# TensorE's order written out from layer C's output projection to block 2's first gate values

## The chip, the core and the metric

One core of one Trainium2 chip runs the whole program, a transformer of two blocks, in one launch. The metric is the device time of one execution in microseconds (us), the median of three runs: 2364.74 us, between 2364.59 and 2366.53. Engines are named as the profile names them: PE (TensorE, the matrix products; PEld its weight loads), DVE (VectorE), ACT (ScalarE), POOL (GpSimd) and SP (SyncE, whose queue issues the loads).

## The reference, cut to what matters

Layer C ends block 1: each head's output is normalised, gated and projected, and a layer norm with a residual follows. Block 2 begins with an RMS norm of the result and projects it; one of the projections gives `zv`, the values of a spatial gate, which go through a GELU and a layer norm.

```python
def hgrn2_readout(o, g, g_norm, w_out):
    on = o * lax.rsqrt(jnp.mean(o * o, axis=-1, keepdims=True) + RMS_EPS) * g_norm
    B, H, L, dv = on.shape
    return (on.transpose(0, 2, 1, 3).reshape(B, L, H * dv).astype(g.dtype) * jax.nn.silu(g)) @ w_out
...
    y = hgrn2_readout(o_f + o_b, g, g_norm, w_out)
    x_new = layer_norm(DEEPNORM_ALPHA * x + gate * y, ln_g, ln_b)
...
        a = rms_norm(h, pre_mix_g[i])
        z = a @ w_in[i]
...
    v = layer_norm_2(jax.nn.gelu(v), ln_g, ln_b)
```

There are 512 tokens, 1024 channels and 8 heads in layer C.

## The kernel before, in words

Activations lie with their channels on the 128 partitions, in 8 tiles k of 128 channels, and the 512 tokens run along the free axis; most work is done in two halves of 256 tokens (`HALVES`). A product is computed in three parts, `mm3` (line 269) and its stepwise form `mm3_steps` (274): each weight and each operand is split into an upper and a lower part, and upper x upper, upper x lower and lower x upper are summed, 3 products for each of the 8 k, so 24 for one output tile of 128 channels. They all carry line 279. `wsplit` (241) loads a weight (line 238, SP's queue), copies its upper part on ACT (246) and takes the lower part on DVE (249). There are 4 buffers for loaded weights and 3 for each split part.

The program is written down in Python and ordered by a list scheduler that simulates the engines: each engine's instructions are put in the order in which the simulation finds them ready, the earlier written first. Inside `with self.tc.manual_schedule(engines={PE})` PE's instructions are prescribed in the order in which they are written; the other engines' are still ordered by the scheduler. Before the change two parts use it: the attention of block 1, and the attention of block 2 with what follows it (`mixer`). There a `_Slots` object (188) holds "sides": generators whose steps are advanced by one at each call `slot(...)`, so that small products come at fixed places between large ones.

The part that changes is `c_out`. `head_out` (line 964) finishes a head of layer C: transposes (975), the states (983, 985), the output products (989 to 991), the head norm (995 to 998), a transpose (1001) and the gate (1002). `c_out` splits the eight heads' outputs into `oh` (line 253 on ACT, 254 on DVE; the profile calls them `hx`). For each half it computes 8 output tiles m; three weights (m = 3, 4, 5) are kept from half 0 in spare buffers (`kw`), so that half 1 starts with these. A result gets its gate and the residual on DVE (1029), and the sum over the tiles is formed on POOL, the last addition on DVE (1031, `total`).

Then come two norms for each half. The layer norm (`layer_norm_steps`, 423): PE's product with a matrix of 1/1024 gives the mean (434, `mu`), DVE subtracts it (439), ACT squares (440), DVE adds the squares (458); `rstd` sums them over channels by 8 small products (312, `rsc`), DVE adds the epsilon (315), POOL takes the power -0.5 (316, `rcol`), PE spreads it over the partitions (320, `rsb`), and DVE multiplies (446). Gain and bias are applied twice: on ACT inside the squares for the next norm (466), and on POOL in place, eight times (1044). The second norm, block 2's RMS norm (`norm_out`), has the same `rstd` chain (312 to 320) and `normed` (1076), which multiplies on DVE (1081) and splits into `self.a`, the upper part on ACT (253), the lower on DVE and POOL in turn (254).

`mixer_in` begins block 2. Its constants are loaded first (lines 1243 to 1255). `token_major` (834) computes the gate values of token tiles 0 and 1, that is of half 0: 4 weights, 2 tiles, 6 products each of 512 columns (line 845), in PSUM tiles `mm`, and `gln_evac` passes them on. `group` (1120) follows: five output tiles of other projections, first for half 0, then for half 1. PE's order in all this is the scheduler's.

Of the kernel before, what the change touches and what calls it, by code (L numbers as in the profile page):

```python
# [10 lines left out]
F32 = mybir.dt.float32  # L11
# [3 lines left out]
AF = mybir.ActivationFunctionType  # L15
ALU = mybir.AluOpType
# [5 lines left out]
ALPHA = 4 ** 0.25  # L22
LN_EPS, RMS_EPS = 1e-5, 1e-6
NORM_EPS = 1e-6
NEG = -1e30
HALVES = [slice(0, 256), slice(256, 512)]
# [152 lines left out]
def now(steps):  # L179

    while True:
        try:
            next(steps)
        except StopIteration as e:
            return e.value
# [21 lines left out]
class _K:  # L207
# [796 lines left out]
    def c_out(self, cp):  # L1004

        nc = self.nc
        nrm = self.nrm
        oh = self.new_x()
        for sl in HALVES:
            for k in range(8):  # L1010
                self.split(oh[0][:, k, sl], oh[1][:, k, sl], self.oy[:, k, sl])
        kept = {}
        kw = [[self.te.tile([128, 1024], F32R, name="kw", tag=t, bufs=b) for _ in range(2)]
              for t, b in (("kqc", 3), ("kq", 2), ("ff", 2))]

        for hf, sl in enumerate(HALVES):
            bank = ("o", "pt")[hf]
            total = cp.tile([128, 256], F32, name="total", tag="total", bufs=2)
            order = range(8)
            if hf:  # L1020
                order = [*kept, *(m for m in range(8) if m not in kept)]
            for i, m in enumerate(order):
                w = (kept.pop(m) if m in kept else self.wsplit(self.d["wo_c"][m])) if hf or not 3 <= m < 6 else None
                if w is None:
                    w = kept[m] = self.wsplit(self.d["wo_c"][m], *kw.pop())
                p = self.big((128, 256))
                self.mm3(p, w, [lambda k, t=t: t[:, k, sl] for t in oh])
                r = self.h[:, m, sl]
                nc.vector.scalar_tensor_tensor(r, p, self.mod[:, 40 + m, 0:1], r, op0=ALU.mult, op1=ALU.add)
                if i:  # L1030
                    (nc.vector if i == 7 else nc.gpsimd).tensor_add(total, total if i > 1 else first, r)
                first = r
            r = self.h[:, :, sl]

            def squares(i, t):
                next(steps)
                for j in range(2):
                    self.gain_bias(r[:, 2 * i + j, :], 2 * i + j, 1, t[:, j, :], AF.Square)

            steps = self.layer_norm_steps(r, 1, cp, lambda k, xn: None, [total], bank, "lq")  # L1040
            next(steps)
            sq = self.sumsq(squares, 256, nrm)
            for k in range(8):
                nc.gpsimd.tensor_scalar(r[:, k, :], r[:, k, :], self.c("ln_g", 8 + k), self.c("ln_b", 8 + k), op0=ALU.mult,
                                        op1=ALU.add)
            self.norm_out(nrm, "pre_mix", 0, sl, sq, bank)


    def norm_in(self, tmp, gain, l, sl, dst=None):
# [175 lines left out]
    def mixer_in(self, l, at, gp, u, qst, kst, kcst, vv, vcz, gt):  # L1225

        nc, d = self.nc, self.d
# [56 lines left out]
        def gln_evac(t, n, p):  # L1284
            x = v[:, t, :]
            self.gelu2(x, p, gp.tile([128, S], F32, name="gmt", tag="gmt", bufs=2))
            bst = gp.tile([128, 6], F32, name="bst", tag="bst", bufs=2)
            mv = gp.tile([128, 2], F32, name="mv", tag="mv", bufs=2)
            nc.vector.bn_stats(bst, x)
            nc.vector.bn_aggr(mv, bst)  # L1290
            nc.gpsimd.tensor_scalar(mv[:, 1:2], mv[:, 1:2], 4 * NORM_EPS, None, op0=ALU.add)
            nc.gpsimd.tensor_tensor(mv[:, 1:2], mv[:, 1:2], self.mhalf[:, 0:1], op=ALU.pow)
            nc.vector.tensor_scalar(x, x, mv[:, 0:1], mv[:, 1:2], op0=ALU.subtract, op1=ALU.mult)
            eng = nc.vector if t < 2 else nc.gpsimd
            eng.tensor_mul(x, x, gln[0])
            eng.tensor_add(x, x, gln[1])

        zv = lambda ts, bank: self.token_major(d[f"w_zv{l}"], 1, lambda k, b, t: self.a[b][:, k, 128 * t:128 * t + 128], ts,
                                               bank, gln_evac)
        zv((0, 1), lambda: self.bk("mm", [128, 512]))  # L1300
        order = (0, 1, 6, 7, 8)
        wgs = [at.tile([128, 192], F32R, name=f"wgs{i}") for i in range(2)]
        self.split(wgs[0], wgs[1], wg)
# [16 lines left out]
        for b in range(2):  # L1320
            k_ = roped(gr[6 + b], 1.0)
            for g in range(2):
                x, y = (slice(0, 64), slice(64, 128)) if g == 0 else (slice(64, 128), slice(0, 64))
# [16 lines left out]
        for r in range(4):  # L1340
            q_ = roped(proj(8 + r) if r else gr[8], 0.125)
            compress(r)
            for g in range(2):
                x, y = (slice(0, 64), slice(64, 128)) if g == 0 else (slice(64, 128), slice(0, 64))
                nc.scalar.copy(qst[x, 2 * r + g, :], q_[x, :])
                nc.vector.tensor_sub(qst[y, 2 * r + g, :], q_[x, :], qst[x, 2 * r + g, :])
        for b in range(2):
            v_ = ev("v_")
            nc.scalar.copy(v_, proj(12 + b))
            p = ptt("vtr", [128, 4, 128])  # L1350
# [6 lines left out]
        p = ptt("htr", [128, 2, 128])  # L1357
# [4 lines left out]
        p = ptt("pkc", [128, 64])  # L1362
# [9 lines left out]
        p = ptt("pvc", [31, 2, 64])  # L1372
# [7 lines left out]
        p = ptt("gtr", [128, 4, 24])  # L1380
# [341 lines left out]
```

## Time and profile before

| | |
|---|---|
| median of three runs | 2364.74 us |
| the profiled execution | 2362.37 us |
| its span, first to last instruction | 2360.5 us |
| PE busy | 2237.1 us |
| DVE busy | 1701.1 us |
| ACT busy | 1140.2 us |
| POOL busy | 519.6 us |
| mean granted PE clock (1 is full speed) | 0.981 |

Times in the rows are microseconds from the span's start unless marked ns. A timeline row gives start, duration, engine, line, operation, out<-in, shape and count; in brackets stands how long the engine sat idle before it and what ended the wait. Consecutive instructions of one kind are merged into one row. PE's products overlap in the pipe, so a row's duration holds the last one's whole length. "PEclk" is the clock that PE was granted: 1.00 is 2.4 GHz, 0.50 is 1.2 GHz.

### The profile page before, as it was taken

Reading aid. Unit: us, or ns where it says so; the run is one execution under the profiler, and the core shown is the slowest. Engines: PE = TensorE matmul, PEld = TensorE weight load, DVE = VectorE, ACT = ScalarE, POOL = GpSimd, SP = SyncE. Lnnn points to the kernel's source line nnn. Section 1 sums busy time; section 2 is a strip of 40 time slices with the busy share of each in tenths; the row PEclk is TensorE's granted clock in tenths of the full one; section 3 lists DMA queues with packets and bytes.
Section 4 is the critical chain, followed back from the end, with each engine's and each line's share of the span. In section 5 each row is a group of like instructions: output and inputs, shape, how many; then the busy total and the mean of one; then the engine's idle time right before and its main releaser. Section 6 shows DMA issues by size and latency. Waiting matters only on the chain.

```text
span 2360.5 us, 37236 instructions
## 1 busy us (share of the span) xinstructions
PE 2237.1 (95%) x14372; PEld 1941.6 (82%) x14372; DVE 1701.1 (72%) x2922; ACT 1140.2 (48%) x2105; POOL 519.6 (22%) x556
## 2 busy tenths in 40 slices
PE   7999999999999989897999999999987999999998
PEld 5877788888888888665898889998865798888998
DVE  5898656846888878776787665668957688666558
ACT  3534444643443434455664444555445665444454
POOL 0110010312444344113121110133203131111004
PEclk9999999999999999998999999999988999999999
DMA  7443134432212344311253235655411143333664
GB/s 286 134 151 99 37 104 132 141 124 82 62 63 63 113 152 130 132 37 46 81 170 105 92 95 157 181 185 163 176 53 45 43 157 126 96 98 112 176 195 134
DMA packets 83746, 279.03 MB, mean 118 GB/s; under 512 B 9584, under 2 KB 14704, under 8 KB 83568
## 3 DMA queue, kind: packets, MB, share of 16 engines
q1 hardware_dynamic: 83568, 276.64, 36.7%
q8 instruction: 113, 1.85, 0.3%
q14 instruction: 65, 0.53, 0.1%
HBM read 274.51 MB, written 2.10 MB: 117 GB/s over the span
## 4 chain that ended last, share of the span: by engine, by line
PE 75%; DVE 13%; ACT 4%; issue 3%; POOL 3%; DMA 2%; SPq 0%; DVEq 0%; ACTq 0%; POOLq 0%
PE mm L279 28%; PE bg L279 23%; PE s L279 3%; DVE wlo L249 2%; PE o L580 2%; PE s L924 2%; PE pt L571 2%; PE bg L845 2%; PE pt L279 1%; PE s L1558 1%; DMA w<-in_w_ada 1%; ACT whi L246 1%; PE s L845 1%; PE bg L1659 1%; DVE ada_p L403 1%
## 5 line engine op out<-in xcount | busy, mean ns | idle before, releaser
L246 ACT CAST whi<-w 128x1024 fp32r<-128x1024 f32 (+1 forms) x436 | 449.1, 1033 | 555.5 <-PE mm L279 249.0
L249 DVE TENSOR_TENSOR wlo<-w,whi 128x1024 fp32r<-128x1024 f32 (+1 forms) x420 | 522.7, 1246 | 223.6 <-ACT whi L246 221.7
L279 PE MATMUL bg<-a,whi 128*128 128x512 f32 x1344 | 415.9, 391 | 0.2 <-ACT whi L246 0.2
L279 PEld LDWEIGHTS bg<-a,whi 128*128 128x128 f32 x1344 | 252.3, 188 | 54.6 <-ACT whi L246 1.0
L279 PE MATMUL mm<-hx,whi 128*128 128x512 f32 x864 | 275.6, 399 | 3.4 <-DVE sga L682 3.0
L279 PE MATMUL bg<-a,wlo 128*128 128x512 f32 x672 | 262.2, 391 | 2.0 <-DVE wlo L249 2.0
L279 PE MATMUL mm<-fh,whi 128*128 128x256 f32 x1408 | 252.7, 282 | 0.0
L279 PEld LDWEIGHTS mm<-fh,whi 128*128 128x128 f32 x1408 | 217.2, 189 | 0.2
L279 PE MATMUL mm<-fh,wlo 128*128 128x256 f32 x704 | 198.9, 284 | 0.6 <-DVE wlo L249 0.6
L279 PEld LDWEIGHTS mm<-hx,whi 128*128 128x128 f32 x864 | 157.9, 190 | 33.1 <-DVE sga L682 3.2
L279 PE MATMUL mm<-a,whi 128*128 128x256 f32 (+1 forms) x768 | 169.8, 317 | 0.0
L279 PE MATMUL mm<-hx,wlo 128*128 128x512 f32 x432 | 169.7, 393 | 0.0
L279 PEld LDWEIGHTS bg<-a,wlo 128*128 128x128 f32 x672 | 126.6, 188 | 29.8 <-DVE wlo L249 3.1
L1611 POOL TENSOR_TENSOR cv<-cv 128x512 f32<-128x512 f32 x44 | 61.5, 1398 | 386.2 <-DVE cv L1598 386.2
L1598 DVE SCALAR_TENSOR_TENSOR cv<-q,cols,cv 128x511 f32<-128x511 f32 (+1 forms) x176 | 134.5, 767 | 2.5
L279 PEld LDWEIGHTS mm<-fh,wlo 128*128 128x128 f32 x704 | 132.6, 189 | 1.0 <-DVE wlo L249 1.0
L279 PEld LDWEIGHTS mm<-a,whi 128*128 128x128 f32 x768 | 124.0, 196 | 7.1 <-issue 4.2
L1605 DVE TENSOR_TENSOR q<-bg,rr 128x512 f32<-128x512 f32 x74 | 51.1, 691 | 107.6 <-PE bg L279 107.6
L279 PE MATMUL mm<-a,wlo 128*128 128x256 f32 (+1 forms) x384 | 117.8, 307 | 0.6 <-DVE wlo L249 0.6
L279 PE MATMUL mm<-hc,whi 128*128 128x256 f32 x576 | 108.6, 287 | 2.3 <-ACT k L813 2.2
L316 POOL TENSOR_TENSOR rcol<-rcol,mhalf 128x2 f32<-128x2 f32 x33 | 24.3, 736 | 348.4 <-DVE rcol L315 348.4
L571 PE MATMUL pt<-ident,p 128*128 128x128 f32 x496 | 72.8, 285 | 29.4 <-DVE p L1577 20.8
(465 smaller groups left out, 4999.8 us busy)
## 6 DMA issues: line engine op xcount, KB each, us to landing
w<-in_wup SPq DMA_DIRECT2D x102, 512.0 KB, 3.5
w<-in_wdn SPq DMA_DIRECT2D x64, 448.0 KB, 3.5
w<-in_w_ada SPq DMA_DIRECT2D x48, 512.0 KB, 3.7
w<-in_w_c SPq DMA_DIRECT2D x48, 512.0 KB, 3.5
w<-in_w_in SPq DMA_DIRECT2D x38, 512.0 KB, 4.7
w<-in_wo SPq DMA_DIRECT2D x32, 512.0 KB, 3.5
w<-in_wdn SPq DMA_DIRECT2D x32, 512.0 KB, 3.6
w<-in_wpg SPq DMA_DIRECT2D x32, 512.0 KB, 3.8
```

The costliest lines, as they stand in the source:

```text
L246: self.nc.scalar.copy(hi[:, :c], w)
L249: eng.tensor_sub(lo[:, :c], w, hi[:, :c])
L279: self.nc.tensor.matmul(ps, w[a][:, (k - k0) * c:(k - k0 + 1) * c], x[b](k), start=first and n == 0, stop=last and n == 3 * len(ks) - 1)
L316: nc.gpsimd.tensor_tensor(col, col, self.mhalf[:, :nt], op=ALU.pow)
L403: nc.vector.scalar_tensor_tensor(t, w, 1.0, self.srow[i], op0=ALU.mult, op1=ALU.mult, accum_out=sums[:, j, i:i + 1])
L571: nc.tensor.transpose(pt[:, c:c + 128], P[g][:, i, kb * 128:(kb + 1) * 128], self.ident)
L580: self.nc.tensor.matmul(o[64 * g:64 * g + 64, 2 * rp:2 * rp + 2, :].rearrange("p a b -> p (a b)"), vt[:, keys[kb], 64 * g:64 * g + 64], pb ...
L845: nc.tensor.matmul(p, xf(k, a, t), w[b][:, 512 * k2:512 * k2 + 512], start=k == 0 and i == 0, stop=k == 7 and i == 2)
L924: nc.tensor.matmul(s_[:, c, :], lhs(c), rhs(c), start=True, stop=True)
L1598: nc.vector.scalar_tensor_tensor(t[:, s:], p[:, :S - s], cw(i), t[:, s:], op0=ALU.mult, op1=ALU.add)
L1605: nc.vector.tensor_mul(q, p, self.rr)
L1611: nc.gpsimd.tensor_mul(a, a, b)
```

## The change

PE's instructions of `c_out` are prescribed, and the gate values of half 0 are moved into that stretch. In each half the tiles' products are written whole, tile by tile and k from 0 to 7, with a slot after every 12 products (`k % 4 == 3`), so two for each tile. After a half its norms become a side, a new generator `norms`. Its first step waits; the next slot gives the mean's product; after the squares four more steps pass; then come the eight small products of the first `rstd`, one slot later its broadcast; after the squares of the second norm five steps pass; then the second `rstd` in two slots. So half 0's norms run through the 16 slots of half 1: mean at slot 1, sums at slot 5, broadcast at 6, sums of the second norm at 11, its broadcast at 12. Half 1's norms run in the 8 slots of the gate values, one after each 6 products; what is left of them (from the second norm's sums on) is written after the prescribed stretch and stays free. The gate values take their weights through `wqueue`, which splits one weight ahead; their PSUM tiles are kept in `self.zv`, and `mixer_in` only calls `gln_evac` on them in the first of block 2's layers. In the second layer nothing changes. The instructions and their number are the same.

```diff
-        for hf, sl in enumerate(HALVES):
-            bank = ("o", "pt")[hf]
-            total = cp.tile([128, 256], F32, name="total", tag="total", bufs=2)
-            order = range(8)
-            if hf:
-                order = [*kept, *(m for m in range(8) if m not in kept)]
-            for i, m in enumerate(order):
...
-                p = self.big((128, 256))
-                self.mm3(p, w, [lambda k, t=t: t[:, k, sl] for t in oh])
...
+        def norms(sl, total, bank):
+
             r = self.h[:, :, sl]
+            pair = lambda i: r[:, 2 * i:2 * i + 2, :]
+            both = lambda t: t[:, None, :].to_broadcast([128, 2, 256])
+            yield
+            mu = self.bk(bank, [128, 256], "mu")
+            nc.tensor.matmul(mu, self.mean1k, total, start=True, stop=True)
+
+            def centred(i, t):
+                nc.vector.tensor_sub(pair(i), pair(i), both(mu))
+                nc.scalar.activation(t, pair(i), AF.Square)
+
+            sq = self.sumsq(centred, 256, cp, "lq")
+            for _ in range(4):
+                yield
+            rs = yield from self.rstd_steps(sq, 256, self.mean1k, LN_EPS / ALPHA ** 2, cp, bank)
 
             def squares(i, t):
-                next(steps)
+                nc.vector.tensor_mul(pair(i), pair(i), both(rs))
                 for j in range(2):
                     self.gain_bias(r[:, 2 * i + j, :], 2 * i + j, 1, t[:, j, :], AF.Square)
 
-            steps = self.layer_norm_steps(r, 1, cp, lambda k, xn: None, [total], bank, "lq")
-            next(steps)
             sq = self.sumsq(squares, 256, nrm)
             for k in range(8):
                 nc.gpsimd.tensor_scalar(r[:, k, :], r[:, k, :], self.c("ln_g", 8 + k), self.c("ln_b", 8 + k), op0=ALU.mult,
                                         op1=ALU.add)
-            self.norm_out(nrm, "pre_mix", 0, sl, sq, bank)
+            for _ in range(5):
+                yield
+            pr = yield from self.rstd_steps(sq, 256, self.mean1k, NORM_EPS, nrm, bank)
+            self.normed(nrm, pr, lambda k: self.h[:, k, sl], lambda k: self.c("pre_mix", k), range(8), sl)
+
+        slot = _Slots()
+        with self.tc.manual_schedule(engines={mybir.EngineType.PE}):
+            for hf, sl in enumerate(HALVES):
...
+                for i, m in enumerate(order):
...
+                    p = self.big((128, 256))
+                    for k, _ in enumerate(self.mm3_steps(p, w, [lambda k, t=t: t[:, k, sl] for t in oh])):
+                        if k % 4 == 3:
+                            slot(0)
...
+                slot.side(norms(sl, total, ("o", "pt")[hf]))
+
+            self.zv = [self.bk("mm", [128, 512]) for _ in range(2)]
+            wq = self.wqueue([self.d["w_zv0"][0, k] for k in range(4)])
+            for kq in range(4):
+                w = next(wq)
+                for t, p in enumerate(self.zv):
+                    for k in (2 * kq, 2 * kq + 1):
+                        for i, (a, b) in enumerate(((0, 0), (0, 1), (1, 0))):
+                            nc.tensor.matmul(p, self.a[a][:, k, 128 * t:128 * t + 128], w[b][:, 512 * (k % 2):512 * (k % 2) + 512],
+                                             start=k == 0 and i == 0, stop=k == 7 and i == 2)
+                    slot(0)
+        for x in slot.sides:
+            now(x)
...
-        zv((0, 1), lambda: self.bk("mm", [128, 512]))
+        if l == 0:
+            for t, p in enumerate(self.zv):
+                gln_evac(t, 0, p)
+        else:
+            zv((0, 1), lambda: self.bk("mm", [128, 512]))
```

## Rows read from the trace of the kernel before

**Rows 1.** The page, part 1: busy us, share of the span, instructions.

```profile
PE 2237.1 (95%) x14372; PEld 1941.6 (82%) x14372; DVE 1701.1 (72%) x2922; ACT 1140.2 (48%) x2105; POOL 519.6 (22%) x556
```

**Rows 2.** Busy time by stretch: the projection, and what follows it.

```profile
core 0: us, PE busy (x) PEld busy (x) DVE busy (x) ACT busy (x) POOL busy (x), PEclk, DMA share, GB/s
839.40:874.60 35.20, 35.13 (x291) 35.00 (x291) 27.72 (x40) 15.55 (x23) 15.91 (x17) 1.00 0.37 113
874.60:893.20 18.60, 8.85 (x32) 6.06 (x30) 16.75 (x27) 7.04 (x15) 16.04 (x17) 0.63 0.50 173
```

**Rows 3.** Timeline of PE, 874 to 892: the products behind a wait.

```profile
876.04 1.02 PE L312 MATMUL rsc<-mean1k,nq 128*128 128x1 f32 x8 [1.32 <-DVE nq L458]
879.11 1.22 PE L434 MATMUL mu<-total,mean1k 128*128 128x256 f32 x2 [2.05 <-DVE total L1031]
883.05 0.69 PE L320 MATMUL rsb<-ident,rcol 128*128 128x128 f32 x2 [2.72 <-POOL rcol L316]
884.75 0.80 PE L845 MATMUL mm<-whi,a 128*128 128x512 f32 x1 [1.01 <-ACT a L253]
...
889.48 1.22 PE L845 MATMUL mm<-whi,a 128*128 128x512 f32 x2 [2.66 <-DVE a L254]
```

**Rows 4.** Busy time in two stretches of 2 us; PEclk is the third number from the end.

```profile
878.00:880.00 2.00, 0.89 (x2) 0.50 (x2) 1.37 (x2) 0.00 (x0) 2.00 (x3) 0.75 0.87 180
...
892.00:894.00 2.00, 2.00 (x12) 1.78 (x12) 1.62 (x3) 0.37 (x1) 1.52 (x3) 0.84 0.00 0
```

**Rows 5.** Timeline of PE where block 2's prescribed attention begins.

```profile
979.36 0.56 PE L1558 MATMUL s<-kst,qst 128*128 128x128 f32 x4
979.75 0.62 PE L1352 MATMUL vtr<-ident,v__9486 128*128 128x128 f32 x4
```

**Rows 6.** Groups of PE's products, 805 to 839.45: those of the projection.

```profile
L279 PE MATMUL bg<-hx,whi 128*128 128x256 f32 x42 | 8.2, 291 | 0.4 <-ACT whi L246 0.3
L279 PE MATMUL bg<-hx,wlo 128*128 128x256 f32 x21 | 5.9, 287 | 0.0
L279 PE MATMUL bg<-hx,kw 128*128 128x256 f32 x42 | 5.4, 285 | 0.0
```

**Rows 7.** Timeline of PE while head 7 is finished.

```profile
822.95 0.60 PE L975 MATMUL pt<-ident,KK 128*128 128x128 f32 x4
...
829.49 2.56 PE L279 MATMUL bg<-hx,kw 128*128 128x256 f32 x20
831.89 0.38 PE L991 MATMUL o<-st,QQ 128*128 128x128 f32 x2
```

**Rows 8.** Timelines of ACT (first row) and DVE, the same stretch.

```profile
825.60 0.58 ACT L977 COPY kt<-pt 128x512 f32<-128x512 f32 x1
...
827.20 1.23 DVE L249 TENSOR_TENSOR kw<-w,kw 128x1024 fp32r<-128x1024 f32 x1
828.34 1.75 DVE L985 SCALAR_TENSOR_TENSOR st<-st,F,pt 128x128 f32<-128x128 f32 x5
```

**Rows 9.** Timelines of PE, DVE and POOL: half 0's norms.

```profile
868.22 0.38 PE L320 MATMUL rsb<-ident,rcol 128*128 128x128 f32 x2
...
875.22 0.68 DVE L458 TENSOR_TENSOR nq<-nq 128x512 f32<-128x512 f32 x1
...
870.59 2.59 POOL L1044 TENSOR_SCALAR h<-h,cols 128x256 f32<-128x256 f32 x3 [3.31 <-ACT nq L466]
873.15 1.20 POOL L1031 TENSOR_TENSOR total<-total,h 128x256 f32<-128x256 f32 x1
874.33 3.58 POOL L1044 TENSOR_SCALAR h<-h,cols 128x256 f32<-128x256 f32 x3
...
878.59 2.31 POOL L1044 TENSOR_SCALAR h<-h,cols 128x256 f32<-128x256 f32 x2
...
882.28 0.72 POOL L316 TENSOR_TENSOR rcol<-rcol,mhalf 128x2 f32<-128x2 f32 x1
```

**Rows 10.** Timeline of SP's queue: loads of the gate values' weights.

```profile
851.72 16.99 SPq L238 DMA_DIRECT2D w<-in_w_zv x4
```

**Rows 11.** Line 1044: durations in ns, shortest/median/longest.

```profile
L1044 POOL TENSOR_SCALAR h<-h,cols x16: 549/982/2062, 870.6 to 908.5; 128x256 f32<-128x256 f32 x16
```

More of the change, by code (lines that the diff above doesn't have):

```diff
@@ L1014, in c_out @@
               for t, b in (("kqc", 3), ("kq", 2), ("ff", 2))]
-        for hf, sl in enumerate(HALVES):
-            bank = ("o", "pt")[hf]
-            total = cp.tile([128, 256], F32, name="total", tag="total", bufs=2)
-            order = range(8)
-            if hf:
-                order = [*kept, *(m for m in range(8) if m not in kept)]
-            for i, m in enumerate(order):
-                w = (kept.pop(m) if m in kept else self.wsplit(self.d["wo_c"][m])) if hf or not 3 <= m < 6 else None
-                if w is None:
-                    w = kept[m] = self.wsplit(self.d["wo_c"][m], *kw.pop())
-                p = self.big((128, 256))
-                self.mm3(p, w, [lambda k, t=t: t[:, k, sl] for t in oh])
[L1028 to L1032, printed above, removed]
-            r = self.h[:, :, sl]
+        def norms(sl, total, bank):
+            r = self.h[:, :, sl]
+            pair = lambda i: r[:, 2 * i:2 * i + 2, :]
[10 more added lines that the diff above has]
+            rs = yield from self.rstd_steps(sq, 256, self.mean1k, LN_EPS / ALPHA ** 2, cp, bank)
             def squares(i, t):
-                next(steps)
+                nc.vector.tensor_mul(pair(i), pair(i), both(rs))
                 for j in range(2):
                     self.gain_bias(r[:, 2 * i + j, :], 2 * i + j, 1, t[:, j, :], AF.Square)
-            steps = self.layer_norm_steps(r, 1, cp, lambda k, xn: None, [total], bank, "lq")
-            next(steps)
             sq = self.sumsq(squares, 256, nrm)
@@ L1045, in c_out @@
                                         op1=ALU.add)
-            self.norm_out(nrm, "pre_mix", 0, sl, sq, bank)
+            for _ in range(5):
[5 more added lines that the diff above has]
+            for hf, sl in enumerate(HALVES):
+                total = cp.tile([128, 256], F32, name="total", tag="total", bufs=2)
+                order = [*kept, *(m for m in range(8) if m not in kept)]
+                for i, m in enumerate(order):
+                    w = (kept.pop(m) if m in kept else self.wsplit(self.d["wo_c"][m])) if hf or not 3 <= m < 6 else None
+                    if w is None:
+                        w = kept[m] = self.wsplit(self.d["wo_c"][m], *kw.pop())
+                    p = self.big((128, 256))
+                    for k, _ in enumerate(self.mm3_steps(p, w, [lambda k, t=t: t[:, k, sl] for t in oh])):
+                        if k % 4 == 3:
+                            slot(0)
+                    r = self.h[:, m, sl]
+                    nc.vector.scalar_tensor_tensor(r, p, self.mod[:, 40 + m, 0:1], r, op0=ALU.mult, op1=ALU.add)
+                    if i:
+                        (nc.vector if i == 7 else nc.gpsimd).tensor_add(total, total if i > 1 else first, r)
+                    first = r
+                slot.side(norms(sl, total, ("o", "pt")[hf]))
[11 more added lines that the diff above has]
+            now(x)
     def norm_in(self, tmp, gain, l, sl, dst=None):
```

## The prediction

> **What bounds the kernel now.** The page comes first: TensorE (PE) is busy 95% of the span [rows 1], so only a stretch where PE is not full can give time back. The busy time by stretch shows one in the code that changes. While layer C's output projection runs PE is full (35.13 of 35.2 us); in the 18.6 us behind it PE works 8.85 us at a mean clock of 0.63 [rows 2]. PE's timeline says why. The products that end half 0's norms and begin half 1's come one at a time, each behind VectorE (DVE), ScalarE (ACT) or GpSimd (POOL). The bracketed idle times are 1.32, 2.05, 2.72, 1.01 and 2.66 us, together 9.8 us [rows 3]. The granted clock fell in this hole: a mean of 0.75 in 878 to 880 puts the fall to half speed at 879.0, and 0.84 in 892 to 894 puts the rise at 892.6 [rows 4]. In these 13.6 us PE waited 6.4 us (the last three waits) and worked about 7.2 us at 1.2 instead of 2.4 GHz, which cost half of that, 3.6 us. **The hole is worth 9.8 + 3.6 = 13.4 us**: all that the change can win here.
>
> **What the order binds.** The change issues the same instructions; only PE's order is prescribed. The kernel has such a stretch elsewhere. In it the attention scores (line 1558, inside the prescribed order) run at 979.36, ahead of a transpose of line 1352 that is written earlier and lies outside it [rows 5]. So prescribed instructions keep their order among themselves, and free ones are put between them as they come ready. The last head's products (lines 975 to 1001) are free and stay where they are; layer C's projection becomes prescribed.
>
> **Cost 1: the work ahead of the last head.** Today the projection does not wait for head 7. Of the first five output tiles the 21 products with k = 0 to 6 (7 k, 3 products each) are already issued while head 7 is being finished: 42 + 21 + 42 = 105 [rows 6]. In the prescribed order tile 0's k = 7 comes 22nd, and it needs head 7's output. So 21 products go ahead and 84 move behind. A group of 20 takes 2.56 us [rows 7]; with 0.28 for the last, that is (2.56 - 0.28)/19 = 0.12 us apart. 84 x 0.12 = **10.1 us move from a covered place to the path**.
>
> Does head 7 come sooner without them? Its last products (lines 989 to 991) start at 831.89, behind a group that ran from 829.49 [rows 7]. Their operand, the state (line 985), is ready at 828.34 + 1.75 = 830.09, and that chain is set by DVE and ACT, not by PE: the copy of the turned keys (line 977) at 825.60 and a weight's lower part (line 249) at 827.20 stand ahead of it in their engines' order [rows 8]. I expect this order to stay, as PE held nothing that these instructions wait for. So head 7 gains 831.89 - 830.09 = **1.8 us**. Bounds: nothing, if the order of the others shifts against it; 5.8 us, if the key copy followed its transposes at once (822.95 + 0.60 = 823.55 [rows 7]): copy 0.58 [rows 8], six products 0.9 (the four transposes' 0.60 x 6/4), three states at 1.75/5 = 0.35 each, so the state is ready at 826.1, which is 4.0 before 830.09, and 4.0 + 1.8 = 5.8. I take 1.8, as every row on the chain but PE's keeps its place.
>
> Without its fillers PE does only short pieces from 823.6 until head 7's output is there. In the hole above the clock fell at 879.0, after a stop at 876.04 - 1.32 = 874.7 and 1.0 us of work in between [rows 3, 4], so I expect it to fall here, and the projection to start at half speed. After the restart at 889.48 PE was at half speed until 892.6 [rows 3, 4], which loses 1.6 us; bounds 0 and 3.6, the hole's own loss. I take **1.6**. Sum of cost 1: 10.1 - 1.8 + 1.6 = 9.9 us.
>
> **Cost 2: a wait at a set place.** In half 1 a slot comes every 12 products, 12 x 0.12 = 1.44 us. The first norm's mean comes at slot 1, its sums at slot 5, its broadcast at slot 6, the second norm's sums at slot 11, its broadcast at slot 12; each is now a fixed point behind which PE's other products queue. Before, the broadcast was done at 868.22 + 0.38 = 868.60 and the last sum of squares at 875.22 + 0.68 = 875.90 [rows 9], 7.3 us later; five slots give 7.2, so slot 11 hardly waits. Slot 12 does. Its broadcast needs POOL's power (line 316), and POOL has eight affines of line 1044 ahead of it: 870.59 (2.0 us after the broadcast) to 878.59 + 2.31 = 880.90, 10.3 us with two additions of line 1031 between them [rows 9]. The power takes 0.72 [rows 9], so it is ready 2.0 + 10.3 + 0.7 = 13.0 us after the broadcast. PE gets there after 7.2 + 1.0 (the eight small products, 1.02 [rows 3]) + 1.44 = 9.6. It waits **3.4 us**, with the rest of half 1 behind it, and half 1's last sum and so its own norms wait too. Bounds: zero with affines near their shortest, and 6.2 (rival 2).
>
> **Cost 3: the smaller set places.** Slots 1, 5 and 6 of both halves. The nearest rows are the waits of the same products today, 2.05 and 1.32 [rows 3]; they were long since DVE and POOL did two things at once. I take **1.8 us** for all six; bounds 0 and 3.4 (both in full).
>
> **Costed at nothing.** The gate values' four weights were issued to SP's queue from 851.72 on, for 17 us [rows 10], ahead of block 2's constants though written behind them, and were there before the gate values began at 884.75 [rows 3]; so writing them ahead of the constants moves them past nothing. If they came later, the gate values would begin later. The products of the gate values, 48, and the norms are the same number. The end of the second half's norms stays free, as before, and is covered by the five tiles that follow; if it came late, those would wait for half 1 of `a`.
>
> **The sum.** Costs 9.9 + 3.4 + 1.8 = 15.1 us against 13.4 us from the hole: **1.7 us slower**. The profiled execution took 2362.37 us (its span 2360.5 and 1.9 around it), so 2364.1 in its terms; the median of the three runs, 2364.74, is 2.4 above it, so **2366.4 us**. A measurement of this kernel can tell about 0.2%, 4.7 us: this is no change.
>
> **A rule on POOL.** First the row: line 1044 takes 549 ns at the shortest, 982 at the median, 2062 at the longest, for one shape [rows 11]. The Trainium skill (SBUF — State Buffer, section Who interferes with whom) says that a VectorE instruction with two SBUF inputs and a GpSimd instruction that reads SBUF share a read interface, so that the later one waits for the whole of the earlier. By that rule the spread in the row is waiting, with which the trace agrees as far as it goes, and the time would be near rival 2's; that price is worked out from rows alone.
>
> **Rivals.**
> 1. *Faster: head 7 really comes sooner.* If ACT and DVE serve head 7 first, cost 1 is 10.1 - 5.8 + 1.6 = 5.9. If besides POOL's affines run near 0.55 us [rows 11], POOL needs 8 x 0.55 + 2 x 1.20 (the addition at 873.15 [rows 9]) = 6.8, its power is ready at 2.0 + 6.8 + 0.7 = 9.5 and slot 12 waits for nothing; with 1.0 for the small places the costs are 6.9, the gain 6.5, the time 2358.2. For it: PE is free for head 7. Against: [rows 8]. Chance 0.22.
> 2. *Slower: GpSimd sets the pace of half 1.* The place is slot 12. Prescribed, half 1 runs its additions beside the affines; three lie among them instead of two. The three affines from 874.33 took 3.58/3 = 1.19 each and the addition before them 1.20 [rows 9]: 8 x 1.19 + 3 x 1.2 = 13.1, so the power comes at 15.8 and PE waits 6.2 us. That is longer than the 4.3 us from the stop to the clock's fall in the hole [rows 3, 4], so 1.6 us more. 1.7 + (6.2 - 3.4) + 1.6 = 6.1 us slower, 2370.8. It decides from the point where the last affine ends over 13 us after the broadcast, when the wait passes 4 us. For it: these affines lay beside a loaded DVE, as they would. Against: the first three, from 870.59, took only 2.59/3 = 0.86. Chance 0.30.
> 3. *The order does less than it says.* The free parts set the end: half 1's `a` comes as late as before and the five tiles wait for it, or PE's order comes out nearly the same. Then 2364.7. Against: the 105 products ahead of time can't stay. Chance 0.05.
>
> The forecast itself has 0.43. **How the numbers follow.** Forecast and rival 3 are within 0.2%: 0.48. Rival 1 gives faster 0.22, rival 2 slower 0.30. The forecast's own range, with costs 2 and 3 between their bounds in part, is 2362 to 2370. The range reaches to rival 1's 2358 and past rival 2's 2370.8 to 2372.5, since the costs' upper bounds (clock 3.6, small places 3.4) can add to it.
>
> **What would show it.** Cost 1: few products of line 279 with `bg<-hx` before head 7's output, some 21, PE idle ahead of lines 991 and 1001, the clock below 1.00 there. Cost 2: one wait of line 320 for POOL `rcol` inside half 1, 2 to 5 us. The hole: no stretch of 18 us with half-busy PE behind the projection. I am wrong if line 991's products start well before 830 on this clock, if that wait is missing, or if PE still idles before the gate values.

## The result: 0.6% slower, 2381.53 us

The changed kernel takes 2381.53 us (median of four runs, 2376.37 to 2383.24); the kernel before, beside it, 2365.64. The ratio is 1.0061, 95% interval 1.0043 to 1.0080. The forecast, 2366.4 with a range up to 2372.5, is wrong: the loss is outside the range.

The first part of the page hardly moves; PE's busy time is 13 us longer than in [rows 1] for the same 14372 instructions, so some of them ran at a lower clock:

```profile
PE 2250.0 (95%) x14372; PEld 1952.8 (82%) x14372; DVE 1699.6 (71%) x2922; ACT 1141.0 (48%) x2105; POOL 519.0 (22%) x556
```

**By stretch.** PE's busy time in the changed kernel (columns: stretch, its length, PE busy with its instructions, granted clock, DMA share, GB/s). The projection, which ran full at 1.00 in [rows 2], now starts behind a half-empty stretch, and its first 15 us have a mean clock of 0.81. The hole of [rows 2] between 875 and 893 is gone (18.47 of 20 us busy), but a new one has opened in the gate values, 895 to 910.

```profile
820.00:840.00 20.00, 10.35 (x65) 0.80 0.57 192
840.00:855.00 15.00, 15.00 (x103) 0.81 0.38 119
855.00:875.00 20.00, 19.03 (x150) 0.95 0.18 53
875.00:895.00 20.00, 18.47 (x142) 0.97 0.33 95
895.00:910.00 15.00, 8.75 (x38) 0.90 0.68 210
910.00:935.00 25.00, 25.00 (x168) 0.85 0.53 155
```

**Head 7.** The groups of the projection's products, 805 to 839.9, are 14 + 7 = 21 where [rows 6] had 105. These are the groups:

```profile
L279 PE MATMUL bg<-hx,whi 128*128 128x256 f32 x14 | 2.7, 290 | 0.0
L279 PE MATMUL bg<-hx,wlo 128*128 128x256 f32 x7 | 2.1, 298 | 0.4 <-DVE wlo L249 0.4
```

PE now stands and waits (its timeline) where [rows 7] showed it working:

```profile
826.68 0.94 PE L983 MATMUL pt<-iv,kt 128*128 128x128 f32 x6 [2.15 <-ACT kt L977]
830.15 0.79 PE L991 MATMUL o<-st,QQ 128*128 128x128 f32 x2 [2.53 <-DVE st L985]
...
838.12 0.63 PE L1001 MATMUL pt<-ident,on 128*128 128x128 f32 x4 [3.34 <-DVE on L998]
839.97 1.04 PE L279 MATMUL bg<-hx,whi 128*128 128x256 f32 x2 [1.22 <-ACT hx L253]
```

The last products of head 7 start at 830.15, 1.7 us before the 831.89 of [rows 7]. But the clock has just fallen, and it falls a second time where the projection begins (the windows of PE again):

```profile
826.00:828.00 2.00, 0.94 (x6) 1.00 0.97 371
828.00:830.00 2.00, 0.00 (x0) 0.63 0.92 320
830.00:834.00 4.00, 3.85 (x18) 0.50 0.54 171
836.00:838.00 2.00, 0.00 (x0) 1.00 0.00 0
838.00:840.00 2.00, 0.66 (x5) 0.69 0.00 0
840.00:844.00 4.00, 4.00 (x17) 0.50 0.17 53
844.00:846.00 2.00, 2.00 (x12) 0.60 0.72 190
```

Two products take 0.79 us instead of 0.38, and head 7's output is there at 839.97, not sooner than the 839.47 of the kernel before (its timeline of PE):

```profile
839.47 0.62 PE L279 MATMUL bg<-hx,whi 128*128 128x256 f32 x3 [1.22 <-ACT hx L253]
```

**Half 1.** POOL's affines and its power (line 1041 is the old 1044) answer to [rows 9] (timeline of POOL):

```profile
877.54 2.18 POOL L1041 TENSOR_SCALAR h<-h,cols 128x256 f32<-128x256 f32 x4 [0.49 <-ACT nq L466]
880.85 5.25 POOL L1041 TENSOR_SCALAR h<-h,cols 128x256 f32<-128x256 f32 x4
886.75 0.71 POOL L316 TENSOR_TENSOR rcol<-rcol,mhalf 128x2 f32<-128x2 f32 x1
```

Beside them DVE did this (its timeline):

```profile
876.11 2.48 DVE L1035 TENSOR_TENSOR h<-h,rsb 128x512 f32<-128x512 f32 x4
...
879.55 1.86 DVE L458 TENSOR_TENSOR nq<-nq 128x512 f32<-128x512 f32 x2
881.33 1.21 DVE L249 TENSOR_TENSOR wlo<-w,whi 128x1024 fp32r<-128x1024 f32 x1
...
883.46 1.21 DVE L249 TENSOR_TENSOR wlo<-w,whi 128x1024 fp32r<-128x1024 f32 x1
```

PE waited at slots 5, 11 and 12 (its timeline):

```profile
871.92 1.02 PE L312 MATMUL rsc<-mean1k,nq 128*128 128x1 f32 x8 [0.97 <-DVE nq L458]
883.68 1.02 PE L312 MATMUL rsc<-mean1k,nq 128*128 128x1 f32 x8 [0.26 <-DVE nq L458]
887.51 0.43 PE L320 MATMUL rsb<-ident,rcol 128*128 128x128 f32 x2 [1.27 <-POOL rcol L316]
```

**The gate values.** They begin at 893.52 and end at 920.6, 27 us for 48 products (timeline of PE; each of the 48 takes 0.23 at full clock, together 11 us). The mean of half 1, at slot 1, waits 3.59 us. Then 24 products of the first free tile of `group` stand between those of the gate values, from 904.93 on, and the first of them that needs the weight's lower part waits 2.57 us for it. The eight sums come only behind them, at 912.87, all at half clock (from 907.9 to 917.5 PE's mean granted clock is 0.51):

```profile
898.67 0.70 PE L1023 MATMUL mu<-total,mean1k 128*128 128x256 f32 x2 [3.59 <-DVE total L1064]
...
908.01 0.58 PE L279 MATMUL s<-a,wlo 128*128 128x256 f32 x1 [2.57 <-DVE wlo L249]
...
912.87 1.70 PE L312 MATMUL rsc<-mean1k,nq 128*128 128x1 f32 x8
...
920.20 0.39 PE L1075 MATMUL mm<-whi,a 128*128 128x512 f32 x1
```

Why the mean waits is read from DVE's timeline. The projection's last product ended at 893.7, but between it and the last addition of the total (898.20) DVE works off two lower parts of weights (1.26 and 1.53) and pieces of half 0's second norm; the last tile's gate and residual (line 1062) run only at 896.02:

```profile
893.96 1.26 DVE L249 TENSOR_TENSOR wlo<-w,whi 128x1024 fp32r<-128x1024 f32 x1
...
896.02 0.47 DVE L1062 SCALAR_TENSOR_TENSOR h<-bg,mod,h 128x256 f32<-128x256 f32 x1
896.41 1.53 DVE L249 TENSOR_TENSOR wlo<-w,whi 128x1024 fp32r<-128x1024 f32 x1
...
898.20 0.41 DVE L1064 TENSOR_TENSOR total<-total,h 128x256 f32<-128x256 f32 x1
```

The kernel before had nearly the same distance: there the mean starts at 879.11 [rows 3], 4.4 us behind the end of the projection at 874.7; here it starts 5.0 us behind.

**Two stretches.** Three moments can be found in every kernel here: the first product with head 7's output (A), the end of the projection's last product (B), and the first prescribed attention scores of block 2 (C; the row at 979.36 in [rows 5]). Differences of their times in each profiled execution, in us; the last column is (ratio - 1) x 2365.6, from the runs:

```
                     A to B    B to C    sum     against before, by the runs
before                35.3     104.6    139.9
after                 53.7     103.0    156.8    +14.4
e1_five_ahead         40.1      97.8    137.9     -4.5
e1_again              41.6      97.9    139.4     -4.7
e2_gate_free          53.7      98.7    152.4    +10.6
e3_both               40.1      98.4    138.5     -2.4
e4_filler             53.7      99.2    153.0    +12.3
e7_ahead_mean4        41.6      98.1    139.7     -2.4
e8_mean4              52.3      98.4    150.7     +9.5
e9_three_ahead        47.7      99.8    147.5     +5.2
e11_ahead_mean3       40.1      99.6    139.8     +0.5
e12_ahead_mean2       41.6     103.3    144.9     +3.8
```

The sums, measured against the kernel before's 139.9, differ from the runs by -0.6 to +4.2 us, most of them by +1 to +2.5, so most of what separates these kernels lies in these two stretches. Each row is one profiled execution; e1_five_ahead and e1_again, one and the same program, differ by 1.5 us in A to B and by 0.1 in B to C. In the changed kernel A to B, the projection, became 18.4 us longer, and B to C, where the whole gain of 13.4 us should have come, only 1.6 us shorter.

### The profile page after: what moved, and what is told of

The parts are those of the page before. It is cut to its first block, busy times and chain, and to the rows that moved or that the text cites. A ratio compares the mean times of both kernels' runs of the same rounds, so it can differ in the third digit from the quotient of the medians.

```text
span 2380.6 us, 37234 instructions
## 1 busy us (share of the span) xinstructions
PE 2250.0 (95%) x14372; PEld 1952.8 (82%) x14372; DVE 1699.6 (71%) x2922; ACT 1141.0 (48%) x2105; POOL 519.0 (22%) x556
## 4 chain that ended last, share of the span: by engine, by line
PE 76%; DVE 12%; ACT 4%; issue 3%; POOL 3%; DMA 2%; DVEq 0%; ACTq 0%; SPq 0%; POOLq 0%
PE mm L279 28%; PE bg L279 24%; PE s L279 3%; DVE wlo L249 3%; PE o L580 2%; PE s L924 2%; PE pt L571 2%; PE bg L845 2%; PE pt L279 2%; PE s L1595 1%; ACT whi L246 1%; PE s L845 1%; PE bg L1696 1%; DMA w<-in_w_ada 1%; PE bg L617 1%
## 5 line engine op out<-in xcount | busy, mean ns | idle before, releaser
L279 PE MATMUL s<-a,whi 128*128 128x256 f32 x512 | 97.2, 289 | 3.4 <-ACT p L1601 1.8
```

What stands on the lines that cost most here:

```text
L279: self.nc.tensor.matmul(ps, w[a][:, (k - k0) * c:(k - k0 + 1) * c], x[b](k), start=first and n == 0, stop=last and n == 3 * len(ks) - 1)
```

## The experiments

All start from the changed kernel.

**Five tiles ahead.** The products with k = 0 to 6 of half 0's first five tiles are written first, as the scheduler had them before; then come their k = 7 and the rest. No slot is called in this part, and half 0 has none to advance.

```diff
+                early = {}
+                for m in range(5 - 5 * hf):
...
+                    p = self.big((128, 256))
+                    early[m] = p, self.mm3_steps(p, w, [lambda k, t=t: t[:, k, sl] for t in oh])
+                    for _ in range(7):
+                        next(early[m][1])
                 for i, m in enumerate(order):
+                    if m in early:
+                        p, steps = early[m]
+                        for _ in steps:
+                            pass
```

> The changed kernel with one thing put back by hand: in half 0 the products with k = 0 to 6 of the first five tiles are written first (105 products), then the k = 7 of each, then the other three tiles. Everything else as changed. Theory A (the prescribed order put 84 products behind head 7 and let the clock fall there): the projection's half 0 ends 11 to 13 us earlier against the changed kernel, the clock stays at 1.00 from 820 to 840, and the time is 10 to 13 us under the changed kernel's 2381.5, so 2368 to 2372. Theory B (the gate values' stretch with half 1's norms at set places is what costs): the time moves by 3 us at most, 2378 to 2382, since what is won early is lost waiting there.

Measured: 2361.70 us, ratio to the kernel before 0.9981 (0.9971 to 0.9991): 19 us gained by one part of the order, more than the 10 to 13 forecast, and both kernels beaten. Run again beside others it gave 0.9980 (0.9969 to 0.9991):

> The same kernel as e1_five_ahead, beside the two others on one chip: 0.997 to 0.9995 of the kernel before, so 2 to 6 us faster.

Its windows show the projection full from the start, and the gate values still with holes:

```profile
820.00:840.00 20.00, 18.11 (x150) 1.00 0.61 203
840.00:855.00 15.00, 14.72 (x119) 1.00 0.52 160
...
875.00:895.00 20.00, 14.01 (x83) 0.97 0.53 172
895.00:910.00 15.00, 14.65 (x83) 0.81 0.42 140
```

A to B fell by 13.6 us (53.7 to 40.1). That is what cutting the five tiles' lead costs in this stretch. B to C fell by 5.2 as well: here the free tile no longer stood among the gate values ahead of the sums, which came 8.6 us behind the mean (14.2 in the changed kernel).

**Gate values and half 1's norms free again**, with and without the five tiles ahead. Both are written as in the kernel before, and the scheduler places their products.

```diff
-                slot.side(norms(sl, total, ("o", "pt")[hf]))
-            self.zv = [self.bk("mm", [128, 512]) for _ in range(2)]
...
+                if not hf:
+                    slot.side(norms(sl, total, "o"))
+        now(norms(sl, total, "pt"))
...
+        zv((0, 1), lambda: self.bk("mm", [128, 512]))
```

> The changed kernel with the gate values and half 1's norms taken out of the prescribed order, written and scheduled as before the change; the projection of both halves with half 0's norms in it stays prescribed. Theory A: the loss ahead of the projection stays, so the time is within 3 us of the changed kernel's 2381.5. Theory B: the 11 us that PE lost between 893.5 and 920.4 (waits of 3.6 and 2.6, half clock from 908 to 917.5) come back, 2370 to 2374. Both together would give 2370 to 2374 here and 2368 to 2372 with the five tiles put back.

> Both of the other edits: five tiles ahead in half 0, and gate values and half 1's norms free; only the projection's order and half 0's norms are prescribed. If A and B each cost what the trace shows and add up: 13 + 11 = 24 us under the changed kernel, 2358, some 7 us under the kernel before. If they overlap (what is early must wait for the norms of half 1): 2364 to 2370.

Measured: 2379.14 us (1.0045, 1.0031 to 1.0059) and 2365.73 us (0.9990, 0.9980 to 0.9999). The first is within 3 us of the changed kernel, as theory A said; the second is the case in which the two costs overlap. The part of the change that orders the gate values costs little by itself: by the ratios, 3.8 us are got back without the five tiles, and with them freeing it is 2 us worse than prescribing it. In both comparisons the intervals overlap, so neither difference is shown. The five tiles' lead is worth 13.0 us here (10.6 against -2.4), and A to B moves by the same 13.6 once more. The profile of e3_both shows what stands in the way of the gain of 13.4 us in this order. Its gate values run without a stop, and a hole as large as the old one stands behind them (a window of PE):

```profile
906.00:919.50 13.50, 4.45 (x27) 0.72 0.45 157
```

Its cause is on PE's timeline, the second norm of half 1:

```profile
914.02 1.83 PE L312 MATMUL rsc<-mean1k,nq 128*128 128x1 f32 x8 [6.41 <-DVE nq L458]
918.50 0.69 PE L320 MATMUL rsb<-ident,rcol 128*128 128x128 f32 x2 [2.64 <-POOL rcol L316]
```

PE is idle for 13.5 - 4.45 = 9.1 us, where the hole of [rows 3] had 9.8. These are half 1's own norms, and PE has run out of half 0's tiles to cover them.

**Is it the clock?** Sixty products into tile 0's bank, whose values the following start overwrites, run ahead of tile 0, so that PE isn't idle while head 7 is finished. No useful product is written at another place.

```diff
+                    for _ in range(60 if not hf and m == 0 else 0):
+                        nc.tensor.matmul(p, w[0][:, 0:128], oh[0][:, 0, sl], start=True, stop=True)
```

> The changed kernel with 60 products more that do nothing for the result (tile 0's first product, each starting anew in the bank that tile 0's sum then begins in), put ahead of tile 0, so that PE is busy while head 7 is finished. No useful product moves ahead. If the clock's fall is a cost of its own (theory A's smaller part), the projection starts at 1.00 instead of 0.50 and head 7's products run at 1.00: 3 to 5 us under the changed kernel, 2376 to 2379. If the clock there only fills time that PE has anyway: within 1 us of 2381.5.

Measured: 2379.17 us, 1.0052 (1.0039 to 1.0066), between the two forecasts and inside the changed kernel's interval. The clock held until 838, then fell all the same (windows of PE), behind the next stop, the same 3.34 us ahead of line 1001 (at 838.87) as in the changed kernel:

```profile
836.00:838.00 2.00, 0.00 (x0) 1.00 0.00 0
838.00:840.00 2.00, 0.63 (x4) 0.87 0.00 0
840.00:844.00 4.00, 3.28 (x14) 0.50 0.21 49
```

A to B stayed at 53.7. Head 7's products did run at full clock, and from the start of line 991 to the output it took 7.7 us (833.03 to 840.72) instead of 9.8. But the filler also stood in their way: thirty of the sixty ran in one group just ahead of head 7's last four transposes of line 975, which started at 827.50 (823.26 in the changed kernel); line 991 started at 833.03 instead of 830.15, and the output came no sooner. So this filler bought nothing that the runs can tell, and what the clock alone costs it does not separate.

**Three tiles ahead**: `range(3 - 3 * hf)` in e1_five_ahead's edit, so 63 products go ahead instead of 105 or 21.

> The changed kernel with the first three tiles' 63 products ahead of head 7's output instead of 21 or 105: 42 products are covered, 42 stay behind it. Theory A (each product moved behind head 7 costs its own 0.12 us, the clock comes on top only where PE stands still): 42 x 0.12 = 5.0 us faster than the changed kernel, 7.8 if the clock also holds (2.8 lost there), so 2373.7 to 2376.5. Rival (it is the full load of PE through head 7 that matters, for the clock, and three tiles don't give it; or the gain of e1_five_ahead comes from another order of the other engines): less than 2.5 us faster than the changed kernel, or over 12.

Measured: 2372.11 us, 1.0022 (1.0009 to 1.0036), 9.2 us under the changed kernel by the ratios: more than the 7.8 forecast, less than the rival's 12. In A to B, which the forecast was about, it gained 53.7 - 47.7 = 6.0 us, and the step to five tiles another 7.6. The price goes with the number of products: 13.6 us for 84, of which 84 x 0.12 = 10.1 are the products and the rest mostly the clock, at the start of the projection and behind the first wait of half 1 (0.86 and 0.71 in the 8 us from 870 in the changed kernel, 1.00 from 858 to 878 in e1_five_ahead). The remainder of its gain, 3.2 us, came in B to C.

**Half 1's mean later.** One number sets at which slot of the gate values it stands: 1 in the change, then 4 without the five tiles, and 4, 2 and 3 with them.

```diff
-            yield
+            for _ in range(4 if bank == "pt" else 1):
+                yield
             mu = self.bk(bank, [128, 256], "mu")
```

> The changed kernel with only half 1's mean three slots later. Theory A: the mean's wait of 3.6 us goes, the free tile no longer stands inside the gate values waiting for its weight (2.6 us, and the half clock after it, 4.8 us lost), 6 to 10 us faster than the changed kernel, about 2373, so still slower than the kernel before, as the 84 products stay behind head 7. Theory B: within 3 us of the changed kernel, as e2_gate_free was.

> Five tiles ahead as in e1_five_ahead, and half 1's mean product at the fourth slot of the gate values instead of the first; its sums then come at the eighth, its broadcast behind the prescribed stretch. Theory A (cost 3 was mis-sized: a set place ahead of its operand holds everything behind it): in e1_five_ahead the mean waited 3.6 us for the total, the sums 2.4 us for DVE's squares, and the clock was at half speed for 6 us after that (3 us lost). All three go, the gate values take about 11 us in a row, and what is gained on PE is given back in part where half 1's a is late: 4 to 6 us faster than e1_five_ahead, about 2357. Theory B (half 1's norms, and not PE's set places, set the end of this stretch, since the five tiles of half 0 cover only 14.4 us): the same time as e1_five_ahead, with the waits moved behind the gate values.

> Five tiles ahead, half 1's mean at the second slot of the gate values. In PE's order as written, 24 products of the gate values and 24 of the free tiles now stand between the mean and its sums, 5.5 + 2.9 = 8.4 us, about the 8.5 us that the squares took behind the mean in e1_five_ahead. Theory (a set place costs what it misses its operand by, on either side: too early PE stands, too late the chain of half 1's norms is drawn out and PE stands at its end): the mean's wait falls from 3.6 to 2.2 us, the sums' from 2.4 to about 0, the clock holds there, and the broadcast comes 3 us sooner than in e1_five_ahead: 2 to 4 us faster than e1_again. Rival (the chain of half 1's norms has its own length, and PE's order in the gate values doesn't matter): within 1.5 us of e1_again.

> Five tiles ahead, half 1's mean at the third slot: 24 products of the gate values and 40 of the free tiles between mean and sums, 5.5 + 4.8 = 10.3 us, so the sums come about 2 us later than they could, and only 14 products are left between the broadcast and the second norm's sums. Theory: the waits ahead of those sums and their broadcast are as in e7_ahead_mean4 (5.5 and 3.5), 0 to 3 us slower than e1_again. Rival (later is better, the mean's wait is all that counts): as fast as e12_ahead_mean2 or faster.

Measured: e8_mean4 2376.42 us, 1.0040 (1.0027 to 1.0052), 5 us under the changed kernel, between its two theories (6 to 10, and at most 3). e7_ahead_mean4 2365.33 us, 0.9990 (0.9978 to 1.0001). On another chip, beside e1_again, e12_ahead_mean2 2370.07, 1.0016 (1.0007 to 1.0024) and e11_ahead_mean3 2366.33, 1.0002 (0.9992 to 1.0011).

In e8_mean4 the mean's wait, the free tile's wait and the half clock in the gate values are gone, as forecast; two other waits, with the clock at 0.50 between them, took their place behind the gate values (timeline of PE):

```profile
925.91 1.84 PE L312 MATMUL rsc<-mean1k,nq 128*128 128x1 f32 x8 [5.48 <-DVE nq L458]
931.46 0.69 PE L320 MATMUL rsb<-ident,rcol 128*128 128x128 f32 x2 [3.71 <-POOL rcol L316]
```

With the five tiles ahead this exchange gains nothing: 97.8 against 98.1 us from B to C, as e7_ahead_mean4's theory B said. The theory that the waits at set places add up, so that slot 2 should be best, is refuted by e12_ahead_mean2, the slowest of the four: 8.5 us slower than e1_again by the ratios, where 2 to 4 faster was forecast, so its rival (within 1.5 us) fell too. The mean of e12_ahead_mean2 waits 2.2 us as forecast, but the other engines' order came out different, and PE waits for weights, and for a bank that DVE had not emptied (two rows of PE's timeline):

```profile
894.91 0.46 PE L279 MATMUL s<-a,wlo 128*128 128x256 f32 x1 [1.96 <-DVE wlo L249]
...
915.07 0.50 PE L279 MATMUL mm<-a,whi 128*128 128x256 f32 x2 [2.78 <-DVE v L262]
```

e11_ahead_mean3 came out 5.2 us slower than e1_again, where 0 to 3 was forecast. The times for slots 1, 2, 3 and 4 (2362, 2370, 2366 and 2365 us, the last from another chip) follow no line. What each order of the free engines costs, and why slot 1's is the best with five tiles ahead, stays open.

## Why the prediction was wrong

**The step that failed: "The hole is worth 9.8 + 3.6 = 13.4 us", entered in full on the side of the gain.** The hole was read rightly, and it is gone. But B to C shrank by only 1.6 us. PE's idle times in this stretch were 11.8 us before, the five of [rows 3] among them, and are 9.8 in the changed kernel, and the half clock costs 4.8 instead of 3.6: what PE won in the hole it lost in the gate values, at a set place that cost 3 had not priced (below). In the forecast's terms B to C came out 10.9 us worse (shorter by 1.6 instead of 13.4 - 0.9, with half of cost 3), A to B 2.4 worse (longer by 18.4 instead of 10.1 + 1.6 + 3.4 + 0.9 = 16.0), and head 7's output 2.3 worse (0.5 later instead of 1.8 sooner). That is 15.6 us, about the miss of 15.1.

Nor did any other order that was tried have the 13.4 us to give: B to C shrank by at most 6.8 (104.6 to 97.8 in e1_five_ahead). What the prediction left out is the row of half 1's own norms, from the total to the last broadcast, which cannot start before the projection ends. From the end of the projection to the start of that broadcast the kernel before took 874.7 to 913.5, 38.8 us, and the changed one 893.7 to 931.1, 37.5 us. In e1_five_ahead it was 880.3 to 912.7, 32.3 us (timelines of PE: before, changed, e1_five_ahead):

```profile
913.51 0.38 PE L320 MATMUL rsb<-ident,rcol 128*128 128x128 f32 x2
931.14 0.38 PE L320 MATMUL rsb<-ident,rcol 128*128 128x128 f32 x2
912.68 0.38 PE L320 MATMUL rsb<-ident,rcol 128*128 128x128 f32 x2
```

In the kernel before, PE's hole lay beside the first part of this row. Where PE's waits in the gate values were taken away (e2_gate_free, e3_both, e7_ahead_mean4, e8_mean4), the row took 37.7 to 37.9 us, and PE, done with its other work, stood still for 9.0 to 9.2 us at its end. The sentence that hid this stands under "Costed at nothing": the end of half 1's norms "is covered by the five tiles that follow". The gate values (11 us) and five tiles of half 0 (120 x 0.12 = 14.4 us) make 25 us of cover for a row of 38. In e3_both the uncovered part is the 9.1 us of idle PE above. In the changed kernel itself the end of the row was covered, since the waits had held the tiles back. The row's length is no constant, as e1_five_ahead's 32.3 shows; that it sets B to C in every order, and what the shortest row would give, is not shown.

**The order binds: right.** 21 products went ahead of head 7, as read from [rows 5].

**Cost 1: the mechanism right, the size low.** Forecast 9.9. A to B gives 13.6 by e1_five_ahead and 12.1 by e1_again, in whose run the clock dipped at the start of the projection; both contain the 1.7 us of clock in half 1 named under cost 3. The 10.1 us for the products hold. Head 7's gain of 1.8 did not reach its output: its products did start 1.7 us sooner, from a state that was ready when forecast, but at half clock, and from their start to the first product that uses the output it was 9.8 us instead of 7.6 (831.89 in [rows 7] to 839.47). The clock at the start of the projection cost half of 840.0 to 845.6, 2.8 us instead of 1.6.

**Cost 2: a wait at the right place, 1.27 us instead of 3.4.** Rival 2's long wait did not occur, though the result has its sign and half of its mechanism occurred. The broadcast was done at 876.1 (875.44 on PE's timeline and 0.63 behind it, at half clock) and the last affine at 886.1, 10.0 us behind it, not the 13 from which that rival decided. One addition (1.07 us) lay between the affines, where the forecast had two and the rival three. The power was there 11.4 us behind the broadcast instead of 13.0, and PE came to slot 12 after 10.2 instead of 9.6. The first four affines took 2.18/4 = 0.55 us, the second four 5.25/4 = 1.31, more than rival 2's 1.19. During the first, DVE ran line 1035, whose second operand, `rsb`, lies where PE wrote it, in PSUM; during the second, it ran additions (line 458) and the lower parts (line 249) with both operands in SBUF. The Trainium skill (SBUF — State Buffer, section Who interferes with whom) says that a VectorE instruction with two SBUF inputs contends with a GpSimd instruction that reads SBUF, and that one with at most one SBUF input, outside the modes that use both ports, does not; the 0.55 and 1.31 us agree with this. The price that the prediction set beside that rule, near rival 2's, did not come: only four of the eight affines ran beside such work. No run changed DVE's work beside the affines alone, so the cause of the 1.31 is argued.

**Cost 3: mis-sized.** In half 1 the two sums wait 0.97 and 0.26 us, within the 1.8. The place not priced was slot 1 of the gate values: 3.6 us for the mean, 2.6 for the free tile that the scheduler set behind it, and 4.8 lost at half clock between 907.9 and 917.5, together 11.0 us. The rows before had it in part: with the mean 4.4 us behind the end of the projection, and slot 1 six products or 1.4 us behind it, the wait comes to 3.0; the forecast took the idle time of 2.05 alone, which had the eight sums of another norm in front of it. In the terms of the sum: A to B grew by 10.1 for the products, 2.8 for the clock, 1.23 + 1.27 for the three waits, 1.7 for the clock behind the first of them (0.86 and 0.71 in the 8 us from 870), and 1.4 for the second norm's small products, which came from the hole into half 1. That is 18.5 against the measured 18.4. A wait of 1.50 us for half 1's `a` (PE at 938.45), which "Costed at nothing" had named as possible, came on top in B to C.

**The rest**: from C to the end the profiled execution takes 2.7 us longer than the one before (1383.9 to 1381.1). Between e1_five_ahead and e1_again, one and the same program, this rest differs by 3.5 us, so nothing is read into it.

**What was not tried**: DVE's order was left to the scheduler throughout, so that the 4.5 us from the projection's end to the total are explained by its timeline alone.

## What to carry to other kernels

Filling a hole on the bounding engine need not give back the hole: here 13.4 us of hole gave 1.6, and at most 6.8 in any order tried. Look for the next dependent chain, measure it from its start to its end, and count the cover that is left for it after the hole's work has been moved, before crediting the hole. Price a set place from the time at which its operand is ready, not from the idle time seen in another order. When an order is written out that a scheduler made before, first list what that scheduler ran ahead of a late operand, and write the same lead into the order; here five tiles' lead was worth 19 us, and 13 with the gate values free, more than anything else that was varied. A single moved product changes the order that the scheduler gives the other engines, so a set place is judged by its run, not by its wait alone.

## What was not expected of the hardware

One program, one order, one wait of 1.22 us ahead of the projection: in one execution PE kept its full clock behind it, in another the mean clock was 0.72 in the 6 us behind it, and A to B was 1.4 us longer (windows of PE below). The Trainium skill (TensorE: Matmul & The Clock Gate, Part 1) says that the number of slow products at a kernel's start varies from run to run; these two executions show the like in the middle of a kernel. This is e1_five_ahead:

```profile
840.00:844.00 4.00, 3.72 (x28) 1.00 0.25 49
844.00:846.00 2.00, 2.00 (x19) 1.00 0.32 63
```

And this is e1_again:

```profile
840.00:846.00 6.00, 5.91 (x35) 0.72 0.17 37
```

Behind the same wait of 0.97 us ahead of half 1's first sums the clock fell in the changed kernel and held in e1_five_ahead, so the 4.3 us from a stop to the fall, on which rival 2 set its price, were one case and no measure.

And the clock rose to 1.00 while PE stood still: in the changed kernel PE does nothing between 836 and 838, behind work at half clock, and the row for it (under **Head 7**) shows 1.00, then 0.69 and 0.50 in the stretches after.
